# Paired score tiles, a bias table that carries its mask, another order of experts and fewer transposes in a two-layer diffusion backbone

## The chip, the cores and the metric

The kernel runs on one core of a Trainium2 chip. The metric is the device time of one execution in microseconds (us), the median of three runs. The profile is of one further execution of the same program.

## The reference, cut to what matters

Two layers act on 256 latent tokens and 256 context tokens of width 1024, in float32. Each layer has attention heads and state-space (SSD) heads side by side, and then a channel mixer: a dense SwiGLU in layer 0, the two best of eight SwiGLU experts in layer 1. In layer 1 only the latent tokens are needed.

```python
# attention, 8 heads of 64; the grid of latent tokens is 4 rows of 64 columns
s_loc = q_row @ k_halo * scale + bias       # learned bias by row and column distance
s_loc = where(in_win, s_loc, -inf)          # a window of 16 columns, clipped at the edges
s_ctx = q_row @ k_ctx * scale
p = softmax(concat([s_loc, s_ctx]))         # context tokens read context only
# experts, width 3584
combine = softmax(top2(h @ router))         # 0 for the six that a token does not take
for e in range(8):
    out += combine[..., e:e+1] * ((silu(h @ wg[e]) * (h @ wu[e])) @ wd[e])
```

The weights of one expert are 3 x 1024 x 3584 float32, 44.04 MB.

## The kernel before, in words

Instructions outside the experts' loop are ordered by a planner that simulates a timeline; there, the order of the code is only a wish. In the experts' loop the order on TensorE is that of the code. DMAs are issued by SP in one queue, in order.

**The mixer** of a layer projects keys, values, queries and the SSD inputs (`mixer`), and then weaves three generators: `attention`, `ssd` and a filler, which in both layers multiplies the modulation weights `w_mod` (2 MB loads `wm`, L266, matmuls L272). One yield of `attention` covers two scores.

`scores` computes for one head and 128 queries the 256 (context) or 512 (latent) scores into a PSUM bank (`s`, L829; the tag S has two banks), adds the bias for the latent keys on VectorE (L833), takes the maximum (L835) and the exponential with its sum on ScalarE (L837). Head h contracts over partitions 0 to 63 or 64 to 127, as h is even or odd. `flip` transposes the result (L845, copied at L846), `values` multiplies it with the values for two heads (L856) and scales.

The bias of a latent head is read from a table in DRAM, `rscr`. `rpb_scratch` fills it: zeros first (L427), and then, when they have landed, eight DMAs (L429), one for each head, that write the 31 biases of each distance for each of 64 columns in a layout whose rows are shifted by one element against each other. `rpb_tile` loads the tile of one head by two DMAs (L439) and adds the window's mask on GpSimd (L440), a sum of 128 x 384 elements. A tile takes part in the scores of two blocks of queries.

**The experts** (`jobs`). A router sorts the experts by their number of tokens: turn 0 is expert 0 and the others follow by rank. Tokens are gathered by a matmul into `xe` (`slots`, L1309). The expert of rank 1, the largest, has 192 slots and is the side job; the others have 64 each, but rank 0 and 7 have 32 and rank 2 has 96 (a tile of 64 and one of 32). A job runs through its 3584 columns in blocks of 1024, 1024, 1024 and 512; the side job in seven chunks of 512 columns, which are put between the blocks at the places that the list `after` names. In a block TensorE does the first half of gate and up (`gu`, L1339), transposes the hidden values of the block before (`flip`, L1406, evacuated at L1410), does the second half, and then multiplies with the down weights of the block before (`y`, for the side job `ys`, both L1339). `act` (L1390, L1391) makes the hidden values, 64 partitions by 512 columns for each 512 columns of gate; the upper 64 partitions of PSUM hold the up half, so that gate and up run beside each other. A job that is done is scaled (`evac`) and brought back to its tokens by `scatter`: for each tile of slots it splits the result in two parts (`split`), multiplies (L1481) and adds four pieces of 128 x 512 on VectorE (L1492), through two PSUM banks.

The weights pass through 15 buffers of 1 MB, in the order of use (`moe_raw`, L1269 and L1277): a load waits until the matmuls of the load 15 places before it are done. The last block of the last job is written out by hand after the loop, with the final norm (`scatter_last`, `last_norm`).

Of the kernel before, what the change touches and what calls it, by code (L numbers as in the profile page):

```python
# [9 lines left out]
F32 = mybir.dt.float32  # L10
# [28 lines left out]
def constants():  # L39
# [27 lines left out]
C_ID, C_LE, C_LT, C_GE, C_GT, C_ONE, C_MASK = 0, 128, 256, 384, 512, 640, 768  # L67
NB = 1
C_COS, C_SIN, C_PERM, C_IOTA, C_TRI8, C_END = 832, 1088, 1344, 1472, 1728, 1792
# [5 lines left out]
class Build:  # L75
# [87 lines left out]
    def setup(self, es):  # L163
# [15 lines left out]
        cA = cst.tile([P, C_MASK], F32, name="cA")  # L179
        nc.sync.dma_start(cA, a["consts"][:, :C_MASK])  # L180
# [426 lines left out]
    def mixer(self, l, m, esm, es_live, mix, fill, before_lat=None, keys=None):  # L607
# [15 lines left out]
        cB = lp.tile([P, C_IOTA - C_MASK], F32, name=f"cB{l}")  # L623
        cmask = cB[:, 0:64]
        lv.update(cos=cB[:, 64:320], sin=cB[:, 320:576], perm=cB[:, 576:704])

        with ExitStack() as es:
# [26 lines left out]
            with self.tc.issue_after(self.last_load.ins):  # L654
                nc.sync.dma_start(cB, a["consts"][:, C_MASK:C_IOTA])
# [45 lines left out]
        with ExitStack() as es:  # L701
            wk = self.pool(es, f"wk{l}", 2)
            self.use_banks(HB, HT)
            self.weave((self.attention(l, wk, qT, kT, v, cmask, mix, tts, q0), 8 * len(tts) // 2 + 1),
# [1166 lines left out]
```

## Time and profile before

| | before |
|---|---|
| median of 3 runs | 1862.05 us (1859.15 to 1862.22) |
| the profiled execution's own time | 1863.58 us |
| its span, first to last instruction | 1861.8 us |
| PE, PEld, DVE, ACT, POOL busy | 95%, 57%, 39%, 26%, 12% of the span |
| mean granted TensorE clock | 0.966 |
| read from HBM | 496.86 MB |

PE is TensorE's matmuls, PEld its weight loads, DVE VectorE, ACT ScalarE, POOL GpSimd, SP the queue that issues most DMAs. L12 is line 12 of the kernel. A tile's name stands without its number. The matmuls of a float32 product are two instructions, and their records overlap, so that a busy share of PE near 100% is no proof that it is the limit; the chain of work that ended last says more. In the stages' times below, layer 0's weave runs from about 184 to 304 us, layer 1's from 868 to 948 us, and the experts from 1005 us to the end.

### The profile page before, as it was taken

Reading aid. Unit: us, or ns where it says so; the run is one execution under the profiler, and the core shown is the slowest. Engines: PE = TensorE matmul, PEld = TensorE weight load, DVE = VectorE, ACT = ScalarE, POOL = GpSimd, SP = SyncE. Lnnn points to the kernel's source line nnn. Section 1 sums busy time; section 2 is a strip of 40 time slices with the busy share of each in tenths; the row PEclk is TensorE's granted clock in tenths of the full one; section 3 lists DMA queues with packets and bytes.
Section 4 is the critical chain, followed back from the end, with each engine's and each line's share of the span. In section 5 each row is a group of like instructions: output and inputs, shape, how many; then the busy total and the mean of one; then the engine's idle time right before and its main releaser. Section 6 shows DMA issues by size and latency. Waiting matters only on the chain.

```text
span 1861.8 us, 25835 instructions
## 1 busy us (share of the span) xinstructions
PE 1776.7 (95%) x10324; PEld 1063.0 (57%) x10324; DVE 724.6 (39%) x1280; ACT 481.2 (26%) x878; POOL 215.1 (12%) x218
## 2 busy tenths in 40 slices
PE   6999998999999999999898999999999999999996
PEld 4787446798989899886465433433433434334332
DVE  4356485772434378677576102011101111110124
ACT  1333544353222235544342111100100101001011
POOL 2000651330000052303312000000000000000000
PEclk8999998999999999999897999999999999999997
DMA  9643893132213212255857999999999999999996
GB/s 329 186 131 127 320 308 114 68 115 87 103 62 132 90 51 93 95 195 201 298 204 293 409 409 412 411 414 411 410 417 409 411 414 414 408 415 356 390 362 263
DMA packets 176160, 499.78 MB, mean 268 GB/s; under 512 B 32520, under 2 KB 43328, under 8 KB 161760
## 3 DMA queue, kind: packets, MB, share of 16 engines
q1 hardware_dynamic: 175008, 496.26, 70.2%
q8 instruction: 83, 1.36, 0.3%
q10 hardware_dynamic: 608, 1.58, 0.2%
q0 software_dynamic: 416, 0.21, 0.1%
q14 instruction: 45, 0.37, 0.1%
HBM read 496.86 MB, written 4.73 MB: 269 GB/s over the span
## 4 chain that ended last, share of the span: by engine, by line
PE 88%; DVE 5%; DMA 4%; ACT 1%; issue 1%; POOL 0%; SPq 0%; DVEq 0%; ACTq 0%; POOLq 0%
PE gu L1339 25%; PE y L1339 9%; PE fm L455 7%; PE fm L454 7%; PE fm L456 7%; PE ys L1339 4%; PE tm L454 3%; PE tm L455 3%; PE tm L456 3%; PE fo L456 2%; PE fo L455 2%; PE fo L454 2%; DMA mg<-in_moe_w_up_dram 2%; PE s L829 2%; PE hT L1406 2%; PE xe L1309 2%
## 5 line engine op out<-in xcount | busy, mean ns | idle before, releaser
L454 PE MATMUL fm<-mhi,uh 128*128 128x512 f32 (+1 forms) x768 | 265.6, 348 | 7.9 <-ACT uh L127 5.5
L455 PE MATMUL fm<-mlo,uh 128*128 128x512 f32 (+1 forms) x768 | 265.8, 347 | 7.2 <-DVE mlo L400 7.2
L456 PE MATMUL fm<-mhi,ul 128*128 128x512 f32 (+1 forms) x768 | 264.6, 346 | 0.0
L455 PEld LDWEIGHTS fm<-mlo,uh 128*128 128x128 f32 x768 | 147.5, 192 | 27.5 <-DVE mlo L400 10.2
L454 PEld LDWEIGHTS fm<-mhi,uh 128*128 128x128 f32 x768 | 146.9, 192 | 28.4 <-ACT uh L127 6.0
L456 PEld LDWEIGHTS fm<-mhi,ul 128*128 128x128 f32 x768 | 147.3, 192 | 18.3 <-DVE ul L132 0.8
L1391 DVE TENSOR_TENSOR ht<-ht,gu 64x512 f32<-64x512 f32 (+1 forms) x47 | 31.6, 673 | 316.7 <-ACT ht L1390 316.5
L1339 PE MATMUL gu<-mg,xes__8789 128*64 128x512 f32 x624 | 149.2, 594 | 1.0 <-DMA mg<-in_moe_w_up_dram 1.0
L1339 PE MATMUL y<-md,hht 128*32 128x256 f32 (+1 forms) x1024 | 150.0, 506 | 0.0
L921 POOL TENSOR_TENSOR mv<-mv,mhalf 128x1 f32<-128x1 f32 x12 | 8.7, 738 | 962.9 <-DVE mv L920 962.6
L1339 PEld LDWEIGHTS y<-md,hht 128*32 128x32 f32 (+1 forms) x1024 | 51.3, 128 | 97.0 <-issue 86.5
L1410 ACT ACTIVATE hht<-hT 128x256 f32<-128x256 f32 (+1 forms) x47 | 17.6, 376 | 336.1 <-PE hT L1406 334.6
L1339 PEld LDWEIGHTS gu<-mg,xes__8789 128*64 128x64 f32 x624 | 48.6, 137 | 87.5 <-issue 83.8
L454 PE MATMUL fo<-uh,hh 128*128 128x256 f32 (+1 forms) x336 | 95.1, 285 | 0.0
L455 PE MATMUL fo<-ul,hh 128*128 128x256 f32 (+1 forms) x336 | 94.8, 284 | 0.0
L456 PE MATMUL fo<-uh,hl 128*128 128x256 f32 (+1 forms) x336 | 92.3, 285 | 0.0
L1391 DVE TENSOR_TENSOR hs<-hs,gu 64x512 f32<-64x512 f32 x21 | 14.5, 689 | 184.7 <-ACT hs L1390 184.7
L1339 PE MATMUL gu<-mg,xet__11435 128*64 128x512 f32 (+2 forms) x416 | 71.2, 565 | 0.0
L455 PEld LDWEIGHTS fo<-ul,hh 128*128 128x128 f32 x336 | 63.2, 188 | 0.8
L454 PEld LDWEIGHTS fo<-uh,hh 128*128 128x128 f32 x336 | 63.0, 188 | 0.8
L1339 PE MATMUL ys<-md,hhs 128*64 128x512 f32 x288 | 63.0, 594 | 0.0
L456 PEld LDWEIGHTS fo<-uh,hl 128*128 128x128 f32 x336 | 62.0, 188 | 0.7
(442 smaller groups left out, 2953.9 us busy)
## 6 DMA issues: line engine op xcount, KB each, us to landing
mg<-in_moe_w_up_dram SPq DMA_DIRECT2D x65, 1024.0 KB, 15.0
mg<-in_moe_w_gate_dram SPq DMA_DIRECT2D x62, 1024.0 KB, 16.8
md<-in_moe_w_down_dram SPq DMA_DIRECT2D x53, 1024.0 KB, 16.5
md<-in_moe_w_down_dram SPq DMA_DIRECT2D x82, 512.0 KB, 11.9
wm<-in_w_mod_dram SPq DMA_DIRECT2D x20, 2048.0 KB, 10.3
mg<-in_moe_w_gate_dram SPq DMA_DIRECT2D x70, 512.0 KB, 11.1
mg<-in_moe_w_up_dram SPq DMA_DIRECT2D x68, 512.0 KB, 12.3
mraw<-in_moe_w_down_dram SPq DMA_DIRECT2D x18, 1024.0 KB, 13.3
```

What stands on the lines that cost most here:

```text
L454: nc.tensor.matmul(ps, ah, bh, start=first and i == 0, stop=False)
L455: nc.tensor.matmul(ps, ah, bl, start=False, stop=False)
L456: nc.tensor.matmul(ps, al, bh, start=False, stop=last and i == n - 1)
L829: nc.tensor.matmul(sv, qT[hp, h // 2, tt * P - q0:(tt + 1) * P - q0], kT[hp, h // 2, :nk * P], start=True, stop=True)
L921: self.last_pow = nc.gpsimd.tensor_tensor(mv[:, 2:3], mv[:, 2:3], self.mhalf[:, 0:1], op=OP.pow)
L1309: nc.tensor.matmul(tp[:, m * W:(m + 1) * W], M["xn"][i][:, j * P:(j + 1) * P], pick[i][:, :, 0:W // n], start=(i == 0), stop=(i == 1))
L1339: self.last_mm = self.nc.tensor.matmul(o[n * g:n * g + n, :w.shape[1]], x, w, start=first, stop=last)
L1391: nc.vector.tensor_tensor(h, h, o[64:, :w], op=OP.mult)
L1406: self.last_flip = nc.tensor.transpose(tp[:, jj * 64:(jj + 1) * 64], h[:, c0:c0 + 255:2], self.ident[:64, :64])
L1410: nc.scalar.activation(t[:, :n], tp[:, :n * 64].rearrange("p (j s) -> p j s", j=n), AF.Copy)
```

## The change

Four edits. The window's mask moves into the table: `rscr` is filled with -1e30, each of eight DMAs writes the 16 biases of the window for the 49 inner columns, and 15 more DMAs write the edge columns; the sum on GpSimd goes. Scores are made for two heads at a time, in one tile of two PSUM banks of which there is one (tag S, bufs 1), with one bias sum and one maximum for both. In the experts' loop two hidden halves share a tile of 128 partitions, which is transposed at once, and in `scatter` tiles of one size are summed in PSUM before the four sums on VectorE. The ranks are taken in another order, and the chunks of the side job stand at other places.

```diff
-    c = np.arange(GRID)
-    start = np.clip(c - WIN // 2, 0, GRID - WIN)
-    inside = (c[None, :] >= start[:, None]) & (c[None, :] < start[:, None] + WIN)
-    mask = np.where(inside, 0.0, NEG).astype(np.float32)
-    cols.append(np.concatenate([mask, mask], axis=0))
...
     def rpb_scratch(self, l):
 
         nc, a = self.nc, self.a
         W = RHD * RW + 1
         flat = self.rscr[l].rearrange("(c x) -> c x", x=W)
-        src = a["na_rpb"][l, :, 4:11, :].rearrange("h r m -> h (r m)").partition_broadcast(64)
+        grid = self.rscr[l][0:64 * RHD * RW].rearrange("(c r w) -> c r w", c=64, w=RW)
+        bias = a["na_rpb"][l, :, 4:11, :]
+        lo, hi = WIN // 2, GRID - WIN // 2 + 1
         with self.tc.issue_after(self.last_load.ins):
-            nc.sync.dma_start(self.rscr[l], a["zeros"])
+            nc.sync.dma_start(self.rscr[l], a["below"])
             for h in range(8):
                 nc.sync.dma_start(
-                    flat[:, h * 7 * RW:(h + 1) * 7 * RW].rearrange("c (r w) -> c r w", w=RW)[:, :, 0:31],
-                    src[:, h, :].rearrange("c (r m) -> c r m", m=31))
-
-    def rpb_tile(self, l, h, pool, cmask):
+                    flat[lo:hi, h * 7 * RW:(h + 1) * 7 * RW].rearrange("c (r w) -> c r w", w=RW)[:, :, 7:23],
+                    bias[h, :, 7:23].partition_broadcast(hi - lo))
+            for c in [*range(lo), *range(hi, GRID)]:
+                k0 = 0 if c < lo else GRID - WIN
+                m0 = k0 - c + 15
+                nc.sync.dma_start(grid[c, :, 15 + k0:15 + k0 + WIN].rearrange("(h r) w -> h r w", h=8),
+                                  bias[:, :, m0:m0 + WIN])
+    def rpb_tile(self, l, h0, pool):
         nc = self.nc
-        t = pool.tile([P, 6, GRID], F32, tag="bias", bufs=3, name=f"bias{l}{h}")
+        t = pool.tile([P, 2, 6, GRID], F32, tag="bias", bufs=2, name=f"bias{l}{h0}")
         flat = self.rscr[l][0:64 * RHD * RW].rearrange("(c r w) -> c r w", c=64, w=RW)
-        for ii in range(2):
-            r0 = h * 7 + 1 - ii
-            nc.sync.dma_start(t[ii * 64:(ii + 1) * 64], flat[:, r0:r0 + 6, 15:79])
-        nc.gpsimd.tensor_tensor(t, t, cmask[:, None, :].to_broadcast([P, 6, GRID]), op=OP.add)
+        for hh in range(2):
+            for ii in range(2):
+                r0 = (h0 + hh) * 7 + 1 - ii
+                nc.sync.dma_start(t[ii * 64:(ii + 1) * 64, hh], flat[:, r0:r0 + 6, 15:79])
         return t
...
+        def scores(lat, tt, h0, bias, sm):
             nk = 4 if lat else 2
-            hp = slice((h % 2) * HD, (h % 2 + 1) * HD)
-            s = self.bank("s")
-            sv = s[:, :nk * P]
-            nc.tensor.matmul(sv, qT[hp, h // 2, tt * P - q0:(tt + 1) * P - q0], kT[hp, h // 2, :nk * P],
-                             start=True, stop=True)
+            self.uid += 1
+            s = self.ps.tile([P, 2, 512], F32, tag="S", bufs=1, name=f"s{self.uid}")
+            for hh in range(2):
+                hp = slice(hh * HD, (hh + 1) * HD)
+                nc.tensor.matmul(s[:, hh, :nk * P], qT[hp, h0 // 2, tt * P - q0:(tt + 1) * P - q0],
+                                 kT[hp, h0 // 2, :nk * P], start=True, stop=True)
             if lat:
                 o0 = 2 if tt == 2 else 0
-                nc.vector.tensor_tensor(sv[:, 256:], sv[:, 256:],
-                                        bias[:, o0:o0 + 4, :].rearrange("p r c -> p (r c)"), op=OP.add)
-            nc.vector.tensor_reduce(sm[:, 0, h:h + 1], sv, AX.X, OP.max, negate=True)
-            p = wk.tile([P, 512], F32, tag="p", bufs=4, name=f"p{l}{tt}{h}")
-            nc.scalar.activation(p[:, :nk * P], sv, AF.Exp, bias=sm[:, 0, h:h + 1],
-                                 accum_out=sm[:, 1, h:h + 1])
-            return p
+                sl = s[:, :, 256:].rearrange("p h (r c) -> p h r c", c=GRID)
+                nc.vector.tensor_tensor(sl, sl, bias[:, :, o0:o0 + 4, :], op=OP.add)
+            nc.vector.tensor_reduce(sm[:, 0, h0:h0 + 2], s[:, :, :nk * P], AX.X, OP.max, negate=True)
+            ps = []
+            for hh in range(2):
+                h = h0 + hh
+                p = wk.tile([P, 512], F32, tag="p", bufs=4, name=f"p{l}{tt}{h}")
+                nc.scalar.activation(p[:, :nk * P], s[:, hh, :nk * P], AF.Exp, bias=sm[:, 0, h:h + 1],
+                                     accum_out=sm[:, 1, h:h + 1])
+                ps.append(p)
+            return ps
...
+                items += [(pair, h0, i) for h0 in range(0, 8, 2) for i in range(2)]
         sms, ps, pTs = {}, {}, {}
-        for n in range(len(items) + 2):
+        for n in range(len(items) + 1):
             if n < len(items):
-                pair, h, i = items[n]
+                pair, h0, i = items[n]
                 lat = pair[0] == 2
                 tt = pair[i]
                 if (tt,) not in sms:
                     sms[(tt,)] = wk.tile([P, 2, 8], F32, tag=f"sm{tt % 2}", name=f"sm{l}{tt}")
                 if i == 0 and lat:
-                    bias = self.rpb_tile(l, h, wk, cmask)
-                ps[n] = scores(lat, tt, h, bias if lat else None, sms[(tt,)])
-            if 0 <= n - 1 < len(items):
-                pair, h, i = items[n - 1]
-                if i == 0:
-                    pTs[h % 2] = self.sp.tile([P, 4, 256], F32, tag="whi", name=f"pT{l}{pair[0]}{h}")
-                flip(pair[0] == 2, h, i, ps.pop(n - 1), pTs[h % 2])
-                if h % 2 and i:
-                    values(pair, h - 1, dict(pTs))
-            if n % 2 == 1:
-                yield
+                    bias = self.rpb_tile(l, h0, wk)
+                ps[n] = scores(lat, tt, h0, bias if lat else None, sms[(tt,)])
+            if n:
+                pair, h0, i = items[n - 1]
+                for hh, p in enumerate(ps.pop(n - 1)):
+                    if i == 0:
+                        pTs[hh] = self.sp.tile([P, 4, 256], F32, tag="whi", name=f"pT{l}{pair[0]}{h0 + hh}")
+                    flip(pair[0] == 2, h0 + hh, i, p, pTs[hh])
+                if i:
+                    values(pair, h0, dict(pTs))
+            yield
...
+            hs, n = [], 0
             for s, two in zip(J["tiles"], os):
                 w = 512 if s == 64 else blk[1] // 2
                 for o in two:
-                    self.uid += 1
-                    h = pj.tile([P, 512], F32, tag="h", bufs=3, name=f"h{J['nm']}{self.uid}")[:64, :w]
+                    if n % 2 == 0 or w < 512:
+                        self.uid += 1
+                        t = pj.tile([P, 512], F32, tag="h", bufs=2, name=f"h{J['nm']}{self.uid}")
+                        hs.append((t, w, []))
+                        n = 0
+                    h = t[n * 64:n * 64 + 64, :w]
                     nc.scalar.activation(h, o[:64, :w], AF.Silu)
                     nc.vector.tensor_tensor(h, h, o[64:, :w], op=OP.mult)
-                    hs.append(h)
+                    hs[-1][2].append(n)
+                    n += 1
             return hs
+            flipped = []
+            for h, w, ns in hs:
+                tp = self.tbank("hT")
+                m, k = 64 * len(ns), w // P
+                for jj in range(k):
+                    c0 = jj // 2 * 256 + jj % 2
+                    self.last_flip = nc.tensor.transpose(tp[:, jj * m:(jj + 1) * m], h[:m, c0:c0 + 255:2],
+                                                         self.ident[:m, :m])
+                self.uid += 1
+                t = pj.tile([P, 4, P], F32, tag="hh", bufs=2, name=f"hh{J['nm']}{self.uid}")
+                nc.scalar.activation(t[:, :k, :m], tp[:, :k * m].rearrange("p (j s) -> p j s", j=k), AF.Copy)
+                flipped += [t[:, :, n * 64:n * 64 + 64] for n in ns]
...
         def scatter(J):
-            for q, (s, y, pT) in enumerate(zip(J["tiles"], J["ys"], J["pT"])):
-                hl = split(y, f"{J['nm']}{q}")
+            for s in (64, 32):
+                qs = [q for q, w in enumerate(J["tiles"]) if w == s]
+                if not qs:
+                    continue
+                hl = [split(J["ys"][q], f"{J['nm']}{q}") for q in qs]
                 for i in range(2):
                     os = [self.tbank("sc") for _ in range(2)]
-                    back(os, s, pT, i, hl, True, True)
+                    for n, q in enumerate(qs):
+                        back(os, s, J["pT"][q], i, hl[n], n == 0, n == len(qs) - 1)
                     for half, o in enumerate(os):
                         hs = slice(half * 512, (half + 1) * 512)
                         nc.vector.tensor_tensor(acc[i][:, hs], acc[i][:, hs], o, op=OP.add)
...
-        after = [(0, 1), (0, 2), (1, 1), (2, 1), (3, 1), (4, 1), (6, 0)]
+        after = [(0, 1), (0, 2), (3, 3), (4, 3), (5, 0), (5, 2), (6, 0)]
...
-                              for p in [3, 4, 5, 6, 2, 7, 1]]
+                              for p in [4, 2, 3, 5, 7, 6, 1]]
                 with tc.issue_after(gate.ins), tc.issue_after(powed.ins), \
                         tc.manual_schedule(engines={mybir.EngineType.PE}):
-                    ranks = [0, 3, 4, 5, 6, 2, 7]
+                    ranks = [0, 4, 2, 3, 5, 7, 6]
                     self.jobs(M, [(turn[t], p, {0: 32, 2: 96, 7: 32}.get(p, 64), bt) for t, p in enumerate(ranks)], J0,
                               (turn[7], 1, 192, bt), self.last_norm)
```

Not shown: the constants and `cB` lose the 64 columns of the mask, the input `zeros` becomes `below`, and `split` has three buffers in place of two.

## Rows read from the trace of the kernel before

**Rows 1.** Windows: start:end, length, busy per engine, PE clock, DMA share, GB/s.

```profile
237.00:304.00 67.00, 63.64 (x347) 34.59 (x346) 50.64 (x116) 31.49 (x83) 27.93 (x30) 0.95 0.68 221
868.00:892.00 24.00, 14.51 (x82) 5.07 (x82) 13.40 (x11) 10.63 (x29) 23.85 (x18) 0.85 0.96 351
892.00:948.00 56.00, 56.00 (x287) 28.32 (x287) 33.86 (x72) 20.45 (x49) 13.81 (x19) 0.94 0.58 195
...
1122.00:1607.00 485.00, 476.04 (x2284) 180.99 (x2282) 66.15 (x132) 49.93 (x106) 0.00 (x0) 0.99 1.03 412
...
1680.00:1740.00 60.00, 59.75 (x450) 22.76 (x453) 4.28 (x9) 6.80 (x16) 0.00 (x0) 0.97 0.93 352
...
1780.00:1800.00 20.00, 19.95 (x164) 8.01 (x166) 2.28 (x4) 1.74 (x4) 0.00 (x0) 0.85 0.81 302
```

**Rows 2.** The chain that ended last, in order of time: start, length, what.

```profile
183.93 1.85 PE mod L272 x16
...
228.95 0.63 PE s L829 x2
...
267.48 1.91 PE s L829 x4
...
1165.39 10.30 PE gu L1339 x48
...
1228.64 1.10 PE hT L1406 x8
...
1247.68 7.02 PE gu L1339 x32
...
1501.01 16.39 DMA mg<-in_moe_w_up_dram
...
1826.48 5.44 PE y L1339 x64
```

**Rows 3.** Instructions on the scores' tile: ns min/median/max, first and last start, forms.

```profile
L835 DVE TENSOR_REDUCE sm<-s x48: 408/678/692, 189.2 to 946.1; 128x1 f32<-128x512 f32 x32, 128x1 f32<-128x256 f32 x16
L837 ACT ACTIVATE p<-s,sm x48: 457/681/688, 190.3 to 946.9; 128x512 f32<-128x512 f32 x32, 128x256 f32<-128x256 f32 x16
L837 ACT ACTIVATION_READ_ACCUMULATOR p<-s,sm x48: 188/193/212, 190.7 to 947.5; 128x1 f32 x48
L833 DVE TENSOR_TENSOR s<-s,bias x32: 410/424/433, 239.1 to 945.6; 128x256 f32<-128x256 f32 x32
```

**Rows 4.** Timeline of TensorE at the side job's scatter: start, length, what.

```profile
1814.26 0.51 PE L1481 MATMUL sc<-yhs,pTs 64*128 64x512 f32 x2
1814.60 0.40 PE L1481 MATMUL sc<-yls,pTs 64*128 64x512 f32 x2
```

**Rows 5.** Timeline at the start of layer 1's weave.

```profile
869.81 1.98 PE L829 MATMUL s<-kT,qT 64*128 64x512 f32 x4
...
883.15 1.45 POOL L440 TENSOR_TENSOR bias<-bias,cB 128x384 f32<-128x384 f32 x1
```

**Rows 6.** Timeline of SP's queue around the two bias tables.

```profile
82.03 6.85 SPq L429 DMA_DIRECT2D rscr<-in_na_rpb_dram  x8
90.41 0.38 SPq L446 DMA_DIRECT2D wv<-in_w_in_dram  x1
...
105.94 7.23 SPq L429 DMA_DIRECT2D rscr<-in_na_rpb_dram  x8
113.27 0.64 SPq L266 DMA_DIRECT2D wm<-in_w_mod_dram  x1
```

**Rows 7.** Instructions on the values' weights in layer 0.

```profile
L127 ACT ACTIVATE uh<-wv x4: 1044/1056/1067, 144.3 to 160.3; 128x1024 fp32r<-128x1024 f32 x4
```

**Rows 8.** Gate and up of the last three experts: first and last start.

```profile
L1339 PE MATMUL gu<-mg,xet__10886 x192: 592/593/644, 1486.4 to 1599.8; 128*64 128x512 f32 x192
L1339 PE MATMUL gu<-mg,xet__11435 x416: 378/592/644, 1607.1 to 1726.9; 128*64 128x512 f32 x65, 128*32 128x512 f32 x52, 128*32 128x256 f32 x22
L1339 PE MATMUL gu<-mraw,xet__12006 x24: 592/592/617, 1738.5 to 1809.5; 128*32 128x512 f32 x24
```

More of the change, by code (lines that the diff above doesn't have):

```diff
@@ L178, in setup @@
         tmp = self.pool(est, "stmp", 1, side="right")
-        cA = cst.tile([P, C_MASK], F32, name="cA")
-        nc.sync.dma_start(cA, a["consts"][:, :C_MASK])
+        cA = cst.tile([P, C_COS], F32, name="cA")
+        nc.sync.dma_start(cA, a["consts"][:, :C_COS])
         self.ident = cA[:, C_ID:C_ID + P]
@@ L622, in mixer @@
                   dte=lp.tile([P, 2, 4, 8], F32, name=f"dte{l}"))
[L623 to L625 removed]
+        cB = lp.tile([P, C_IOTA - C_COS], F32, name=f"cB{l}")
+        lv.update(cos=cB[:, 0:256], sin=cB[:, 256:512], perm=cB[:, 512:640])
         with ExitStack() as es:
@@ L703, in mixer @@
             self.use_banks(HB, HT)
-            self.weave((self.attention(l, wk, qT, kT, v, cmask, mix, tts, q0), 8 * len(tts) // 2 + 1),
+            self.weave((self.attention(l, wk, qT, kT, v, mix, tts, q0), 8 * len(tts) // 2 + 1),
                        (self.ssd(l, wk, lv, dtt, mix, tts), 7 + 6 * len(tts)),
@@ L873, in attention @@
             if pair[0] in tts:
-                items += [(pair, h, i) for h in range(8) for i in range(2)]
+                items += [(pair, h0, i) for h0 in range(0, 8, 2) for i in range(2)]
         sms, ps, pTs = {}, {}, {}
-        for n in range(len(items) + 2):
+        for n in range(len(items) + 1):
             if n < len(items):
-                pair, h, i = items[n]
+                pair, h0, i = items[n]
                 lat = pair[0] == 2
@@ L1391, in act @@
                     nc.vector.tensor_tensor(h, h, o[64:, :w], op=OP.mult)
-                    hs.append(h)
+                    hs[-1][2].append(n)
+                    n += 1
             return hs
         def flip(J, blk, hs):
-            out, hs = [], iter(hs)
-            for s in J["tiles"]:
-                hT = []
-                for _ in range(blk[1] // 512 if s == 64 else 1):
-                    h = next(hs)
-                    n = h.shape[1] // P
-                    tp = self.tbank("hT")
-                    for jj in range(n):
-                        c0 = jj // 2 * 256 + jj % 2
-                        self.last_flip = nc.tensor.transpose(tp[:, jj * 64:(jj + 1) * 64], h[:, c0:c0 + 255:2],
-                                                             self.ident[:64, :64])
-                    self.uid += 1
-                    t = pj.tile([P, 4, 64], F32, tag="hh", bufs=4, name=f"hh{J['nm']}{self.uid}")
-                    nc.scalar.activation(t[:, :n], tp[:, :n * 64].rearrange("p (j s) -> p j s", j=n), AF.Copy)
-                    hT.append(t)
+            flipped = []
@@ L1412, in flip @@
+            out = []
+            for s in J["tiles"]:
                 if s == 64:
+                    hT = [flipped.pop(0) for _ in range(blk[1] // 512)]
                     out.append(lambda t, odd, hT=hT: hT[t // 2][:, t % 2 * 2 + odd, :])
                 else:
-                    m = n // 2
-                    out.append(lambda t, odd, hT=hT, m=m: hT[0][:, t % m * 2 + odd, t // m * 32:t // m * 32 + 32])
+                    hT, m = flipped.pop(0), blk[1] // 512
+                    out.append(lambda t, odd, hT=hT, m=m: hT[:, t % m * 2 + odd, t // m * 32:t // m * 32 + 32])
@@ L1855 @@
     arrays, aps = {}, {}
-    for name in _INS + ["consts", "zeros"]:
+    for name in _INS + ["consts", "below"]:
         if name == "consts":
             arr = constants()
-        elif name == "zeros":
-            arr = np.zeros(64 * (RHD * RW + 1), np.float32)
+        elif name == "below":
+            arr = np.full(64 * (RHD * RW + 1), NEG, np.float32)
         else:
```

14 lines of the change are left out of this document (6 added, 8 removed).

## Prediction, made before the changed kernel ran

> **What bounds the kernel now.** I read the chain of waits that ended last first, then the windows by stage, then the tiles that the change touches.
>
> The chain [rows 2] is TensorE nearly throughout. In the experts its last DMA is the one at 1501.01 us; from there to the end it holds TensorE and, at the scatters, VectorE. The windows show the other side [rows 1]: from 1122 to 1607 us the DMA share is 1.03 at 412 GB/s. The experts are thus balanced between two limits. One expert's 44.04 MB take 44.04 / 0.412 = 106.9 us, a side chunk's 6.29 MB take 15.3 us, together 122.2 us; TensorE's period for a 64-slot expert with one chunk is 1607.1 - 1486.4 = 120.7 us [rows 8]. After 1607 us the balance breaks. The expert with 96 slots takes 1738.5 - 1607.1 = 131.4 us [rows 8] for 106.9 us of weights, its buffers fill, and the DMA rate falls to 352 GB/s over 60 us and to 302 GB/s over 20 us [rows 1]. That is (412 - 352) / 412 x 60 = 8.7 us and (412 - 302) / 412 x 20 = 5.3 us of transfers, 14.0 us in all.
>
> In the weaves TensorE is busy too, but at the start of layer 1's it works 14.51 of 24 us while GpSimd works 23.85 [rows 1]. Its first scores are begun at 869.81 us, and the first sum of the mask on GpSimd comes at 883.15 us [rows 5].
>
> **Scores in pairs.** Two latent score products stand at 1.91 us in the chain, 0.955 us each, and one context product at 0.63 us [rows 2]. Before, neighbours in the order are two blocks of queries of one head, on the same half of the array. After, they are an even and an odd head, on different halves. The nearest row for that is the scatter: two half-height matmuls take 0.51 us together and the next two end 0.74 us after the first began [rows 4], where the second pair's record alone is 0.40 us, so the two of a pair run beside each other. If that holds here, a pair costs what one did: 8 x 0.955 + 8 x 0.63 = 12.7 us less TensorE work in layer 0, 8 x 0.955 = 7.6 us in layer 1. The lower bound is 0, if they queue.
>
> The price is the one score tile. The next pair's product must wait until both exponentials of this pair are done. The sum grows from 0.424 to about 0.69 us (256 more columns cost 0.678 - 0.408 = 0.27 us in the maximum's two forms), the maximum to 0.678 + 2 x 0.27 = 1.22 us, the exponentials are 2 x (0.681 + 0.193) = 1.75 us [rows 3]. With the product of 0.95 us this is 4.6 us; I take 5 us with the hand-offs. Layer 0's latent half has 67 / 8 = 8.4 us for a pair, layer 1 after 892 us has 56 / 8 = 7.0 us [rows 1]. So the chain of a pair fits, but not with much room in layer 1, and transposes, values, SSD and modulation matmuls must fill the gap. VectorE saves about 0.3 us a pair.
>
> **The mask.** It takes the sum on GpSimd away, 1.45 us for the first [rows 5], less where GpSimd is alone. In layer 0, where GpSimd works 27.93 of 67 us [rows 1] and VectorE is ahead of it, the slack covers it: 0; without that cover it would be the 1.45 us of each of eight sums. In layer 1 the first softmax no longer waits behind GpSimd's queue; of the 24 - 14.51 = 9.5 us in which TensorE is idle there I take 4, bounds 0 and 9.5, because SSD's own sums hold GpSimd too.
>
> **The tables.** 15 more DMAs are issued by SP for each layer, at 6.85 / 8 = 0.86 us [rows 6], so 12.9 us. The values' load moves from 90.41 to 103.3 us; its weights are first used at 144.3 us [rows 7]. The first `wm` behind the second table moves from 113.27 to 139 us; its matmuls are at 183.93 us [rows 2]. Cost 0, hidden by these 45 us. One head more of bias loads than before goes ahead of the `wm` loads at each weave's start, since two pairs are fetched in place of three heads: two DMAs, 1 to 2 us, taken off below.
>
> **Sum of the weaves.** Layer 0: 12.7 us of TensorE work less, of which I let 8 through, since VectorE works 50.64 of 67 us there [rows 1] and the pair's chain passes it twice. Layer 1: 7.6 + 4 - 1.6 = 10 us. Bounds: 0 and 12.7, 0 and 17. What they save moves all that follows, and so the weight stream of the experts.
>
> **Transposes and scatter.** Eight transposes take 1.10 us, 0.1375 each [rows 2]. Three blocks of 1024 columns need four in place of eight for each 64 slots, 3 x 4 x 0.1375 = 1.65 us for each of five experts; a chunk eight in place of twelve, 0.55 us for each of seven: 12 us less TensorE work, if a transpose of 128 rows costs what one of 64 does. The side job's scatter runs from 1814.26 to 1826.48 us [rows 4, 2], 12.2 us, because twelve sums on VectorE through two banks hold TensorE. Four are left; I take half, 6 us. Both count only where TensorE, not the DMA, is last.
>
> **The order.** A chunk is 144 matmuls, 48 of which take 10.30 us [rows 2], and 12 transposes: 30.9 + 1.65 = 32.6 us. So a 64-slot expert alone is 120.7 - 32.6 = 88.1 us, 86.4 after. Half the matmuls of one, 1.75 blocks of 3 x 7.02 us [rows 2], is 36.9 us; with the 11 us that remain of the 88.1, an expert with 32 slots is about 50 us. The ledger after, TensorE against DMA: second expert 86 to 107, so TensorE waits and the buffers hold no backlog; the 96-slot one 130 to 107, 23 behind; the next two with a chunk 118 to 122, 4 won back each; the 32-slot one with two chunks 114 to 138, 23 won back; the last with a chunk and the side job's scatter about 117 to 122. Fifteen buffers are 15.7 MB, 38 us of transfers, so 23 us of backlog can be taken up in the middle, and nothing is behind at the end. Of the 14.0 us of lost transfers I take 11 back: 1.5 us go to a last expert of 64 slots (its last two loads are 16 matmuls, 3.5 us, in place of half that), 1.5 us to a brim in the 96-slot expert. Bounds 0 and 17, the latter with some of the scatter's saving at the end.
>
> **The sum.** 8 + 10 + 11 = 29 us off the profiled execution's own 1863.58 (its span is 1861.8, 1.8 around it): 1834.6. The median shown is 1.5 us lower, 1862.05, so I say 1834. A change under 0.2%, 3.7 us, can't be told from none here.
>
> **Rivals.**
>
> *The one score tile becomes the limit, slower (chance 0.11).* It decides from 7.0 us a pair in layer 1 and 8.4 us in layer 0. At 9 us, with a VectorE instruction of others ahead of the sum and of the maximum, the cost is 8 x 2.0 = 16 and 8 x 0.6 = 5 us in place of the 18 saved: 1862.05 + 21 - 11 = 1872. For it: VectorE's 50.64 of 67 us. Against it: 5 us without a queue. What would make it bite is that the waiting product holds back what stands behind it on TensorE. The Trainium skill (TensorE: Matmul & The Clock Gate, section Part 3: Packing small matmuls) has matmuls start and end strictly in program order; by that rule every wait for the tile is a wait of the whole queue. No row here shows a matmul that overtook another.
>
> *Only the experts gain (0.14).* The weaves stay on VectorE, GpSimd and the `wm` loads: 1862 - 11 = 1851.
>
> *Only the weaves gain (0.09).* The 96-slot expert fills the buffers in the middle as it did late, and the chunks after it keep them full: 1862 - 18 = 1844.
>
> *The tables come late (0.05).* If a write takes 2.1 us in place of 0.86, 23 take 48 us: the first table ends at 130, the second at about 194 us, and the first `wm` is issued there, 10 us after its use, and needs at least 2.1 MB / 0.412 = 5 us more: 1834 + 15 = 1849. The Trainium skill (DMA: Bandwidth & Descriptors, section Why a DMA increments its semaphore by 16 and not by 1) lets a DMA use the largest number of engines up to 16 that divides its slowest dimension; the 49 columns would go over 7 engines where 64 went over 16, which is how a write could become that slow. The rows have no transfer of 49.
>
> *It does nothing that can be measured (0.05).* 1862.
>
> **How the numbers follow.** The forecast itself has 0.56: its own range is 1817, with all bounds on the good side, to 1848, with half of the sum. The range of 8 in 10 goes on to the cases at 1849 and 1851, with their own spread, and leaves out the slow one and the best end: 1817 to 1856. Faster 0.83 (0.56 + 0.14 + 0.09 + 0.04 of the late tables), same 0.06, slower 0.11.
>
> **What would show it.** Right: latent score products of a pair in 1 us or little more, layer 1's first exponential before 882 us counted from the same start, no window of the experts under 400 GB/s before the last 20 us, and a scatter of the side job of some 6 us. Wrong: TensorE waiting for ScalarE's exponential ahead of scores for more than some 10 us in sum, a second `wm` wait at layer 0's start, or a DMA rate that falls in the 96-slot expert and the chunks behind it.

## The result and the profile after

The changed kernel takes 1830.67 us (median of 4 runs, 1829.24 to 1832.0) where the kernel before takes 1861.88 (median of 4): ratio 0.9835, interval [0.9818, 0.9852], 31 us less. The profiled execution takes 1831.6 us, its span is 1829.8, the mean clock 0.973 (0.966 before).

Windows of the changed kernel for those of [rows 1]. The three of the weaves begin 5 us ahead of their counterparts, since the marks come earlier there; those of the experts stand at the same times as before, and the one from 1620 to 1680 us is added:

```profile
232.00:299.00 67.00, 57.96 (x357) 32.53 (x357) 50.70 (x103) 33.18 (x85) 24.32 (x26) 0.97 0.72 242
863.00:887.00 24.00, 16.53 (x99) 7.10 (x99) 16.21 (x15) 13.03 (x35) 23.04 (x18) 0.90 1.00 332
887.00:934.00 47.00, 45.70 (x290) 25.54 (x290) 31.81 (x62) 20.05 (x50) 8.19 (x12) 0.98 0.81 274
1122.00:1607.00 485.00, 469.66 (x2572) 168.70 (x2569) 65.89 (x124) 46.84 (x91) 0.00 (x0) 0.98 1.03 413
1620.00:1680.00 60.00, 54.77 (x422) 22.55 (x420) 5.88 (x12) 6.42 (x14) 0.00 (x0) 0.91 1.03 410
1680.00:1740.00 60.00, 57.87 (x280) 19.47 (x278) 10.68 (x17) 4.46 (x8) 0.00 (x0) 0.97 1.03 411
1780.00:1800.00 20.00, 19.12 (x98) 7.63 (x98) 3.95 (x6) 1.57 (x4) 0.00 (x0) 1.00 1.03 416
```

TensorE is busy for 57.96 of 67 us in layer 0's half (63.64 before), layer 1's weave after its start is through in 47 us (56 before), and the dips to 352 and 302 GB/s are gone. The chain of waits of the changed kernel, the pieces that answer to [rows 2]:

```profile
1138.75 19.59 DMA md<-in_moe_w_down_dram
...
1172.29 18.88 DMA mg<-in_moe_w_up_dram
...
1227.96 1.30 PE hT L1419 x8
...
1628.90 17.27 DMA mg<-in_moe_w_up_dram
...
1695.24 11.13 DMA mg<-in_moe_w_up_dram
...
1780.31 1.64 PE sc L1497 x12
1783.28 1.67 PE sc L1497 x10
1784.94 7.02 PE y L1349 x32
```

TensorE waits for weights in the second expert and again at 1628.90 and 1695.24 us, the last of them until 1706; before, the last such link ended at 1517 [rows 2]. So the weights set the pace until 189 us later than before. The side scatter takes 1780.31 to 1784.94, 4.6 us (12.2 before), and a transpose of 128 rows 1.30 / 8 = 0.16 us (0.1375 with 64).

### The profile page after: what moved, and what is told of

It reads as the page before. It is cut to its first block, busy times and chain, and to the rows that moved or that the text cites. A ratio compares the mean times of both kernels' runs of the same rounds, so it can differ in the third digit from the quotient of the medians.

```text
span 1829.8 us, 25533 instructions
## 1 busy us (share of the span) xinstructions
PE 1734.6 (95%) x10236; PEld 1037.4 (57%) x10236; DVE 712.8 (39%) x1232; ACT 476.2 (26%) x856; POOL 203.3 (11%) x202
## 4 chain that ended last, share of the span: by engine, by line
PE 84%; DMA 7%; DVE 5%; ACT 1%; POOL 1%; issue 1%; SPq 0%; DVEq 0%; ACTq 0%; POOLq 0%
PE gu L1349 24%; PE y L1349 8%; PE fm L460 7%; PE fm L459 7%; PE fm L461 7%; PE ys L1349 4%; DMA mg<-in_moe_w_up_dram 3%; PE tm L459 3%; PE tm L460 3%; PE tm L461 3%; DMA wm<-in_w_mod_dram 2%; PE fo L461 2%; PE fo L460 2%; PE fo L459 2%; PE xe L1319 2%; PE hT L1419 1%
## 5 line engine op out<-in xcount | busy, mean ns | idle before, releaser
L1349 PE MATMUL gu<-mg,xes__8731 128*64 128x512 f32 x600 | 141.6, 603 | 2.1 <-DMA mg<-in_moe_w_up_dram 1.2
L1423 ACT ACTIVATE hht<-hT 128x512 f32<-128x512 f32 (+2 forms) x32 | 15.0, 473 | 306.4 <-PE hT L1419 306.4
L1349 PEld LDWEIGHTS gu<-mg,xes__8731 128*64 128x64 f32 x600 | 44.7, 139 | 85.5 <-issue 78.9
L1349 PE MATMUL ys<-md,hhs 128*64 128x512 f32 x264 | 59.3, 605 | 0.0
```

The source lines that it names most:

```text
L1349: self.last_mm = self.nc.tensor.matmul(o[n * g:n * g + n, :w.shape[1]], x, w, start=first, stop=last)
L1423: nc.scalar.activation(t[:, :k, :m], tp[:, :k * m].rearrange("p (j s) -> p j s", j=k), AF.Copy)
```

## The experiments

The table gives, for each run, the ratio to the kernel before and the interval, and from its profiled execution (us) the start of layer 0's last exponential, of layer 1's first, of the router's maximum, of the second expert's first matmul, the last weight load issued, and the end of the span. Runs with the same weave differ by up to 4 us in such a mark, so means over them are used below.

| run | ratio | L0 last | L1 first | router | 2nd expert | last load | end |
|---|---|---|---|---|---|---|---|
| before | 1 | 296.8 | 889.7 | 986.3 | 1121.7 | 1822.5 | 1861.8 |
| changed | 0.9835 [0.9818, 0.9852] | 292.8 | 873.0 | 967.3 | 1096.3 | 1785.9 | 1829.8 |
| e1 order alone | 1.0065 [1.004, 1.009] | 298.6 | 888.5 | 985.0 | 1120.5 | 1812.5 | 1865.8 |
| e2 transposes, scatter | 0.9986 [0.9971, 1.0001] | 299.5 | 886.1 | 982.0 | 1116.3 | 1814.1 | 1855.0 |
| e3 mask | 0.9928 [0.9907, 0.9948] | 298.1 | 874.9 | 971.4 | 1101.7 | 1803.6 | 1843.7 |
| e4 pairs | 0.9971 [0.9952, 0.9989] | 293.0 | 886.2 | 978.8 | 1113.9 | 1811.4 | 1850.4 |
| e5 e1 and e2 together | 0.9939 [0.9924, 0.9954] | 299.0 | 889.8 | 986.0 | 1120.2 | 1808.0 | 1851.5 |
| e6 changed, old order | 0.9858 [0.9842, 0.9875] | 291.9 | 871.5 | 966.0 | 1095.2 | 1793.0 | 1833.2 |
| e7 changed, 32 slots last | 0.9836 [0.9823, 0.9849] | 293.2 | 873.0 | 967.7 | 1096.7 | 1790.8 | 1831.1 |
| e8 changed, old scatter | 0.9879 [0.9864, 0.9893] | 293.1 | 873.0 | 967.6 | 1096.7 | 1786.4 | 1837.0 |
| e9 sums held | 0.999 [0.9978, 1.0003] | 298.5 | 886.5 | 982.5 | 1112.6 | 1815.0 | 1854.3 |
| e10 mask, other sums | 0.9924 [0.9911, 0.9936] | 297.3 | 874.6 | 970.7 | 1101.1 | 1802.9 | 1842.2 |
| e11 same half | 0.993 [0.9917, 0.9944] | 301.5 | 882.4 | 983.8 | 1112.9 | 1802.3 | 1846.1 |
| e12 spread | 0.9835 [0.9811, 0.9858] | 294.3 | 875.3 | 969.5 | 1098.6 | 1791.2 | 1829.2 |

**The parts one by one, on the kernel before.** e1 takes these lines of the diff alone:

```diff
-        after = [(0, 1), (0, 2), (1, 1), (2, 1), (3, 1), (4, 1), (6, 0)]
+        after = [(0, 1), (0, 2), (3, 3), (4, 3), (5, 0), (5, 2), (6, 0)]
...
-                    ranks = [0, 3, 4, 5, 6, 2, 7]
+                    ranks = [0, 4, 2, 3, 5, 7, 6]
```

> The kernel before with nothing changed but the order of the experts and the places of the side chunks. Theory (the order recovers the lost transfers): the DMA rate has no dip to 352 and 302 GB/s any more, and of the 14.0 us of lost transfers about 11 come back, less what the old scatter takes at the end, so 8 to 11 us faster, 1851 to 1854. Rival (the experts' gain after is less TensorE work from transposes and scatter, and the order only moves the wait from one expert to another): within 3 us of before.

Measured: 12 us slower (7 to 17). Neither theory held. In the profiles the stream, from the first expert's matmul to the last load issued, is 9 us shorter (991.7 to 1812.5, 820.8 us; before 992.9 to 1822.5, 829.6), but the tail, from there to the end, is 14 us longer (53.3 for 39.3). That makes 5 us and not 12, since the profile before is long in its experts: e3, e4, e9 and e10, which have the same experts, take 825.8 and 39.4 us on average. Against them e1's stream is 5 us shorter and the whole 9 us longer. The rates show that part of the dips came back in the middle, windows of e1:

```profile
1500.00:1560.00 60.00, 59.80 (x302) 24.23 (x300) 5.74 (x14) 7.11 (x16) 0.00 (x0) 1.00 1.02 402
1620.00:1680.00 60.00, 58.13 (x445) 23.80 (x446) 7.04 (x13) 6.82 (x15) 0.00 (x0) 1.00 0.98 390
```

and its chain has the last wait for weights here, so that TensorE sets the end from 1732 us on:

```profile
1720.90 11.16 DMA mg<-in_moe_w_up_dram
...
1819.72 8.24 PE y L1339 x32
```

e2 takes `act`, `flip`, `split` and `scatter` of the change alone:

```diff
-                for i in range(2):
-                    os = [self.tbank("sc") for _ in range(2)]
-                    back(os, s, pT, i, hl, True, True)
+                    for n, q in enumerate(qs):
+                        back(os, s, J["pT"][q], i, hl[n], n == 0, n == len(qs) - 1)
```

> The kernel before with nothing changed but the transposes of two halves at once and the side tiles summed in PSUM. Theory: these count only where TensorE is last. From 1607 us on in the kernel before it is, and there lie the scatter (12.2 us, 4.6 in the changed kernel) and some 1.35 + 2 x 0.3 us of transposes; 8 to 10 us faster at most, 1852 to 1854, and little on top of the new order. Rival (transposes and scatter run beside VectorE and DMA waits that stay): within 3 us of before.

Measured: 2.6 us less (0 to 5), the rival's size. In the kernel before TensorE holds the chain from 1517 us on, so a shorter scatter should count there. But in e2 TensorE comes through the scatter early and then waits for the last weights. Its waits from 1800 to 1835 us (us in total, times, longest):

```profile
PE y L1339 <- DMA md<-in_moe_w_down_dram: 2.3, 2, 1.4
PE y L1339 <- DMA mraw<-in_moe_w_down_dram: 2.0, 2, 1.3
PE gu L1339 <- DMA mg<-in_moe_w_up_dram: 1.0, 1, 1.0
```

That is 5.3 us of the 7.6 that the scatter is shorter; the kernel before has no such wait there. The stream keeps its dips in the old order (373 GB/s over 1680 to 1740 us) and ends no sooner.

e3 takes the mask table, with single scores:

```diff
-        nc.gpsimd.tensor_tensor(t, t, cmask[:, None, :].to_broadcast([P, 6, GRID]), op=OP.add)
```

> The kernel before with nothing changed but the mask written into the table, so that GpSimd adds none; scores one by one in two score tiles as before. Theory (both weave parts count, the mask only at layer 1's start): layer 0 unchanged, layer 1's first exponential 4 to 8 us earlier, 4 to 5 us faster in all, about 1857. Rival (the mask alone makes the weaves' gain, because GpSimd's queue held the first softmax and the wait ran through the whole of layer 1): 12 us or more faster, 1850 or less. Second rival (GpSimd's sums of SSD hold the first softmax anyway): within 2 us.

Measured: 13 us faster, the rival's size. Layer 1's first exponential comes 14.8 us earlier and the router's maximum 14.9; layer 0 is unchanged.

e4 takes the paired scores, with the mask still on GpSimd:

```diff
+        nc.gpsimd.tensor_tensor(t, t, cmask[:, None, None, :].to_broadcast([P, 2, 6, GRID]), op=OP.add)
```

> The kernel before with nothing changed but the scores of two heads at once in one tile; the mask is still added on GpSimd, one sum of 128x768 for a pair, and the first pair waits for it. Theory (paired products free TensorE in both layers): 5 us in layer 0, 6 to 8 us in layer 1 less 1 to 2 us because the first mask sum is twice as long, in all 9 to 12 us faster, 1850 to 1853. Rival (the paired scores gain nothing without the mask table, since GpSimd's sum stands before each pair): within 3 us of before or slower.

Measured: 5.4 us faster (2 to 9), between theory and rival. Layer 0 has its 5 us; what layer 1 gains does not stand out of the spread of the marks.

The four parts alone sum to +0.65 - 0.14 - 0.72 - 0.29 = -0.50%, 9 us; together they give -1.65%, 31 us. So some of them depend on each other.

**Together, and one at a time out of the changed kernel.** e5 is the kernel before with the edits of e1 and e2:

> The kernel before with the new order, the transposes of two halves and the summed scatter together; the weaves are those of before. Theory (they only pay together: the order shortens the weight stream by some 9 us but leaves a last expert of 64 slots and the side scatter behind it, 53 us from the last weight load issued to the end in place of 39; transposes and scatter take that tail back): from the first expert's matmul to the end 856 us as in the changed kernel, where the kernel before took 869 and the order alone 874; about 13 us faster, 1847. Rival (the terms add, +5 and -3): within 4 us of before.

Measured: 11.4 us faster (9 to 14), the theory: +12 and -3 become -11. From the last load issued to the end 43.5 us are left of e1's 53.3. e6 is the changed kernel with the first lines of e1's diff as they stand before:

> The changed kernel with the order of the experts and the places of the chunks of before. Theory (with short transposes and the short scatter the new order is worth 866 - 856 = 10 us, by the experts' time of the run with these two alone): 8 to 11 us slower than the changed kernel, about 1840. Rival (the order is worth nothing or costs, as alone): 1825 to 1833.

Measured: 4.3 us slower than the changed kernel (0.9858 against 0.9835), half of the theory's. With the new scatter and transposes the order gains; with the old ones it costs. As in e2, TensorE waits for the last weights, 5.7 us from 1780 us on. e8 puts the old `split` and `scatter` into the changed kernel:

> The changed kernel with the side tiles scattered one by one as before. Theory (the side scatter lies in the tail, where TensorE is last, and took 12.2 us against 4.6): 7 to 8 us slower than the changed kernel, 1838. Rival (the tail has room for it, or the weight stream is last): within 2 us of the changed kernel.

Measured: 8.2 us slower (0.9879 against 0.9835), the theory. Timeline of TensorE in e8: the first of six such pairs, the start of the second, which waits for VectorE's sums, and the end of the last:

```profile
1778.26 0.50 PE L1497 MATMUL sc<-yhs,pTs 64*128 64x512 f32 x2
1778.60 0.40 PE L1497 MATMUL sc<-yls,pTs 64*128 64x512 f32 x2
1780.49 1.10 PE L1497 MATMUL sc<-yhs,pTs 64*128 64x512 f32 x2 [1.50 <-DVE res L1508]
...
1789.24 1.21 PE L1497 MATMUL sc<-yls,pTs 64*128 64x512 f32 x2
```

Nothing that issues weights is held up there: the last load leaves at 1786.4 us, 812.2 after the first expert's matmul, as in the changed kernel (811.9). From it to the end it takes 50.6 us in place of 43.9.

**Two other orders.** e7 exchanges the last two experts of the changed kernel:

```diff
-                    ranks = [0, 4, 2, 3, 5, 7, 6]
+                    ranks = [0, 4, 2, 3, 5, 6, 7]
```

> The changed kernel with the last two experts exchanged, so that the 64-slot one with two chunks comes first and the 32-slot one with one chunk is last. Theory (what is left of the experts is the tail: 44 us from the last weight load issued to the end, of which an expert of 32 slots would need some 10 less): the weight stream keeps its 411 GB/s, TensorE waits for weights in the last expert, and the kernel is 5 to 10 us faster than the changed one, 1821 to 1826. Rival (the 64-slot expert with two chunks, 86 + 62 = 148 us of TensorE for 138 us of weights, fills the buffers and the stream stalls before the last expert): within 3 us of the changed kernel or slower.

Measured: as the changed kernel, the rival. From the last load to the end it takes 40.3 us, 3.6 less, but the 64-slot expert with two chunks fills the buffers, and the stream takes 816.4 us in place of 811.9. Windows of e7:

```profile
1560.00:1620.00 60.00, 58.41 (x275) 20.05 (x271) 8.08 (x12) 4.53 (x8) 0.00 (x0) 1.00 0.97 386
...
1680.00:1740.00 60.00, 60.00 (x314) 20.48 (x312) 7.64 (x11) 5.44 (x11) 0.00 (x0) 1.00 0.97 385
```

e12 exchanges them too and moves chunks, so that the second expert has one:

```diff
-        after = [(0, 1), (0, 2), (3, 3), (4, 3), (5, 0), (5, 2), (6, 0)]
+        after = [(0, 1), (0, 2), (1, 1), (3, 3), (4, 3), (5, 1), (6, 0)]
```

> The changed kernel with the order of experts in which the second one, where TensorE waits for weights, gets a chunk, the expert with 32 slots is last, and none has two chunks but the first: no expert after the one of 96 slots is heavier on TensorE than on the weights, and the last has 86 us of work for 122 us of weights. Theory (the weight stream at its full rate, some 812 us from the first expert's matmul to the last load issued, and 40 us behind it as in the run with the 32-slot expert last): 1824 to 1828, 2 to 6 us faster than the changed kernel. Rival (the 96-slot expert now meets full buffers, since TensorE no longer waits ahead of it, and the stream stalls there): the changed kernel's 1830 or slower.

Measured: 0.9835 again, with a wider interval. Its experts take 853.1 us in place of 855.8 in the profiles, less than the runs can tell. In e7 and e12 TensorE waits for weights 8.2 and 11.7 us from 1750 us on, in the changed kernel 0.5 us from 1690 us on: there the stream sets the end. No version run here beats the changed kernel.

**Why the mask table gains in layer 1.** e10 is e3 with other sums on GpSimd, meant to stand in place of the mask's:

```diff
+        nc.gpsimd.tensor_tensor(self.junk, self.cA[:, 0:384], self.cA[:, 0:384], op=OP.add)
```

> The kernel with the mask table and single scores, as in the third run, and in place of each mask sum a GpSimd sum of the same size, 128x384, into a tile that nothing reads. Theory (layer 1's first softmax waited for the mask sum that stood behind SSD's in GpSimd's queue): the first exponential of layer 1 stays at 875 to 878 us and the router's maximum at 972 to 975, where before they are at 889.7 and 986.3. Rival (the gain is GpSimd's time, which SSD needs): they go back to 885 or later and 982 or later. The first expert's period, 123.7 us in the third run, says in either case whether GpSimd's last sums meet the routing again.

Measured: 0.9924 and 874.6 us, the whole gain. But the run does not decide between theory and rival. Nothing waits for these sums, and the planner put all 16 at the start of the kernel, far ahead of the weaves; the row of e10:

```profile
L446 POOL TENSOR_TENSOR junk<-cA x16: 826/828/1787, 7.2 to 34.6; 128x384 f32<-128x384 f32 x16
```

So e10 is e3 a second time, and the question is left to the timelines. VectorE's at the first bias sum, in the changed kernel:

```profile
864.17 3.81 DVE L787 TENSOR_TENSOR E<-E 128x512 f32<-128x512 f32 x2 [1.79 <-POOL E L775]
870.94 0.70 DVE L840 TENSOR_TENSOR s<-s,bias 128x512 f32<-128x512 f32 x1 [2.95 <-DMA bias<-rscr]
871.67 1.23 DVE L841 TENSOR_REDUCE sm<-s 128x2 f32<-128x1024 f32 x1
```

and in the kernel before:

```profile
879.69 2.37 DVE L783 TENSOR_TENSOR E<-E 128x512 f32<-128x512 f32 x1 [6.78 <-POOL E L771]
...
887.34 0.75 DVE L833 TENSOR_TENSOR s<-s,bias 128x256 f32<-128x256 f32 x2
```

Now VectorE waits only for the table's rows, 6 us after the first score product (864.9); before, the sum came 17.5 us after it, behind SSD's sums and the mask. GpSimd's second pair of SSD sums in the kernel before:

```profile
877.77 3.75 POOL L771 TENSOR_TENSOR E<-E,cs 128x1024 f32<-128x1024 f32 x2
```

and in e3:

```profile
876.74 3.74 POOL L773 TENSOR_TENSOR E<-E,cs 128x1024 f32<-128x1024 f32 x2
```

Up to these sums GpSimd does the same work in both, 1.0 to 1.1 us apart; the first mask sum of the kernel before follows at 883.15 us [rows 5], and e3 has its first exponential at 874.9 us. So the early first softmax is not GpSimd's time: it no longer stands behind other work. The eight mask sums of this weave are 8.8 us of GpSimd's time, and how much of the gain behind the first softmax comes from them, no run separates.

**What a pair's products are worth.** e11 lets both products of a pair read the lower half.

```diff
-                hp = slice(hh * HD, (hh + 1) * HD)
+                hp = slice(0, HD)
```

> The changed kernel, with both score products of a pair read from the lower half of the partitions, so that the second repeats the first's head and half of the heads are left out. Theory (the two products of a pair run beside each other because they are on different halves of the array): two latent products take 1.1 us in place of some 0.6, the weave of layer 0 ends 3 to 5 us later, layer 1's 0 to 4 us, 1834 to 1838 in all. Rival (layer 0's gain comes from fewer and longer VectorE instructions, not from TensorE): within 2 us of the changed kernel.

Measured: 17.7 us slower than the changed kernel (0.993 against 0.9835), more than either. The 1.1 and 0.6 us expected for two products were both too small. One latent pair in TensorE's timeline, in the changed kernel:

```profile
269.63 1.13 PE L835 MATMUL s<-kT,qT 64*128 64x512 f32 x4
```

and in e11:

```profile
269.81 1.98 PE L835 MATMUL s<-kT,qT 64*128 64x512 f32 x4
```

So the two halves run beside each other, 0.85 us saved a latent pair: 13.6 us for 16 pairs. Eight context pairs add 3.4 us (1.13 us for a pair in e11, 0.70 in the changed kernel). Against the mean of the five runs with the changed weave (293.1, 873.2, 967.6) layer 0 ends 8.4 us later and layer 1's part behind it takes 16.2 - 8.4 = 7.8 us more. About all that TensorE does longer comes out at the end.

**The first expert.** In the kernel before it takes 1121.7 - 992.9 = 128.8 us, in the changed one 122.3. VectorE's timeline in the kernel before:

```profile
993.14 1.30 DVE L1230 TENSOR_TENSOR sw<-oh,ci 128x64 f32<-128x64 f32 x1
994.36 0.15 DVE L1245 TENSOR_TENSOR cap<-cap,few 128x8 f32<-128x8 f32 x1
994.47 0.22 DVE L1231 TENSOR_REDUCE key<-sw 128x8 f32<-128x64 f32 x1
994.61 1.11 DVE L1244 TENSOR_SCALAR few<-rank 128x8 f32<-128x8 f32 x1
```

and GpSimd's:

```profile
991.72 2.63 POOL L1803 TENSOR_TENSOR res<-xn,res 128x512 f32<-128x512 f32 x2 [6.77 <-PE xe L1309]
994.43 2.61 POOL L1803 TENSOR_TENSOR res<-res,res 128x512 f32<-128x512 f32 x2
```

The routing, on which SP waits for the next weights, is drawn out while GpSimd's sums run. e9 holds these back until the routing is done:

```diff
+                    held = nc.gpsimd.tensor_copy(hold, self.routed[:, 1])
...
-                        with tc.issue_after(self.last_pooled.ins):
+                        with tc.issue_after(held.ins):
```

> The kernel before, with the eight GpSimd sums of the last layer's residual held behind the end of VectorE's routing by one small copy on GpSimd that reads the routing's last result. Theory (in the kernel before these sums begin 5.4 us after the router's maximum and VectorE's routing instructions then take 1.06 to 1.30 us in place of 0.15 to 0.22; in the changed kernel the sums begin 9.0 us after it, when the routing is nearly done, by the luck of a later transfer): the routing ends some 6 us earlier, SP issues the next weights 5 to 6 us earlier, the first expert's period falls from 128.8 to 122 or 123 us, and the kernel is 5 to 6 us faster, 1856. Rival (the long instructions wait for something else, and the changed kernel's short first period comes from the weight stream): within 2 us of before.

Measured: the first expert's period falls to 123.5 us as expected, but the time only by 0 to 4 us, nearer to the rival's. VectorE in e9, with GpSimd waiting:

```profile
990.12 0.16 DVE L1245 TENSOR_SCALAR few<-rank 128x8 f32<-128x8 f32 x1
990.24 0.22 DVE L1237 TENSOR_TENSOR sw<-oh,comb 128x64 f32<-128x64 f32 x1
```

What e9 gains at the start it gives back late, where full buffers stop the stream (346 GB/s over 1660 to 1700 us, 378 before): e4, whose first expert takes 128.5 us, needs 865.0 us from that expert's first matmul to the end, e9 865.2. With the old order and the old scatter the end is TensorE's; the chain of e9 has no wait for weights after 1508 us.

## Why the prediction came out, step by step

**Weaves, 8 and 10 us: right in sum, wrong in their parts.** Over the five runs with the old weave the three marks are 298.5, 888.1 and 984.4 us, with the changed one 293.1, 873.2 and 967.6: layer 0 gives 5.4, layer 1 another 11.4, together 16.8 for 18 forecast. The products on two halves are worth what "Scores in pairs" said: 8 let through in layer 0 (8.4 by e11) and 7.6 in layer 1 (7.8). The step that failed is the price of pairing, which "So the chain of a pair fits" set at 0. The pairs as a whole give 5 us in layer 0 (e4) and nothing in layer 1 (e3 and e10 reach the router's maximum 13.3 us early, the changed weave 16.8, and 5.4 of that is layer 0's). So pairing costs about 3 and 8 to 10 us beside what the products give.

The windows show the price as idle time of TensorE. Layer 0's weave, before and after:

```profile
184.00:304.00 120.00, 114.14 (x622) 57.42 (x617) 79.55 (x171) 57.23 (x164) 60.82 (x63) 0.96 0.77 264
184.00:300.00 116.00, 102.03 (x631) 52.32 (x630) 80.22 (x151) 59.63 (x170) 56.12 (x55) 0.97 0.80 274
```

TensorE is busy 12.1 us less, near the 12.7 of the prediction, but idle 14.0 us in place of 5.9. Layer 1 from the first score to the router, with the mask table and single scores (e3) and in the changed kernel:

```profile
867.00:971.00 104.00, 96.89 (x536) 56.56 (x536) 72.78 (x149) 47.38 (x106) 32.57 (x34) 0.98 0.85 288
863.00:967.00 104.00, 91.68 (x537) 54.88 (x536) 71.71 (x133) 47.25 (x107) 33.69 (x34) 0.97 0.85 300
```

Here TensorE is busy 5.2 us less and idle 5.2 us more, so nothing is left. What it waits for in the changed kernel (us in total, times, longest), in layer 0 and then in layer 1:

```profile
PE pT L855 <- ACT p L846: 5.8, 5, 2.3
...
PE st L726 <- POOL xe L722: 3.9, 2, 2.6
PE pT L855 <- ACT p L846: 2.7, 3, 1.3
```

In layer 0 the transposes `pT` wait 5.8 us for the exponentials (1.4 before). In layer 1 a product of SSD, `st`, waits 3.9 us for GpSimd's `xe`, which it does not in e3, and the transposes 2.7 (1.4 in e3). The next pair's scores wait for ScalarE only 1.7 us in both layers. So the wait that the prediction priced, for the tile, is small, and the cost lies in what comes behind the scores. Whether the pairs' longer instructions or the planner's new order make these waits stays open. In layer 1 a pair takes (930.1 - 873.0) / 7.5 = 7.6 us in the changed kernel, over the 7.0 from which that rival decides; by single scores two take 6.8 (874.9 to 925.6, e3), but e3 then needs 45.8 us more to the router's maximum, the changed kernel 37.2. The rule of the Trainium skill beside that rival (TensorE: Matmul & The Clock Gate, section Part 3: Packing small matmuls), strict program order, was not tested: no run tells where a waiting product held back others.

**The mask, 4 us in layer 1 with bounds 0 to 9.5: mis-sized, and over its bound.** It is worth 13.3 (e3, e10). The bound took TensorE's idle time at the start, but the first softmax came 11.5 us too late, and what hangs on it (transposes, values, SSD between them) followed. From the first score to the router in the kernel before:

```profile
868.00:986.00 118.00, 104.17 (x537) 58.58 (x536) 74.42 (x149) 48.23 (x107) 40.72 (x42) 0.93 0.76 273
```

In e3, above, TensorE is idle 6.7 us less (7.1 for 13.8), and its matmuls, as many, take 7.3 us less at a granted clock of 0.98 in place of 0.93. For the clock the sum had no term. The two errors, mask too small and pairs too good, cancel; that the weaves' sum came out is luck.

**Tables, 0: right.** SP's queue in the changed kernel:

```profile
82.19 6.85 SPq L428 DMA_DIRECT2D rscr<-in_na_rpb_dram  x8
89.09 10.27 SPq L434 DMA_DIRECT2D rscr<-in_na_rpb_dram  x15
99.46 0.39 SPq L451 DMA_DIRECT2D wv<-in_w_in_dram  x1
...
130.49 0.39 SPq L261 DMA_DIRECT2D wm<-in_w_mod_dram  x1
```

A write of 49 columns is issued in 6.85 / 8 = 0.86 us, as one of 64 was [rows 6], and an edge write in 10.27 / 15 = 0.68 us; `wv` goes at 99.46 and `wm` at 130.49, 45 and 53 us ahead of 144.3 and 183.93 [rows 7, 2]. Over how many DMA engines a write of 49 columns goes, the rule of the Trainium skill weighed there (DMA: Bandwidth & Descriptors, section Why a DMA increments its semaphore by 16 and not by 1), no run shows.

**Experts, 11 us: right as a sum, 11.4 by e5; the step that failed is where it comes from.** The order was to recover 11 us of lost transfers by itself and the shorter scatter and transposes to count little. By e1 the order alone costs 12: the stream is 5 to 9 us shorter, and "1.5 us go to a last expert of 64 slots" was 14 with the old scatter behind it and still 4 to 5 with the new (43.5 us in e5, 43.9 in the changed kernel, 39.3 before). TensorE sets the end from 1732 us on in e1, so there the scatter's 7.6 us (8.2 by e8) and the transposes count. Only with them is the order a gain of 4 to 9 us (e6; e5 against e2), and only with the order are they more than 2.6 us (e2). The remark that scatter and transposes "count only where TensorE, not the DMA, is last" was right, and not followed to its end: the new order makes that place, while in the old one TensorE waits for the last weights as soon as the scatter is short.

**The signs.** All four came: 1.13 us a latent pair, the first exponential at 873.0 us, no window of 60 us behind 1020 us under 400 GB/s, a scatter of 4.6 us (6 said, so the saving is 7.6 in place of 6). Of the signs of being wrong none came. The chain has a second `wm` link in layer 0, at 224.75 us, but TensorE does not wait for it: it is busy all 20 us from 220 to 240.

## What to carry to other kernels

A reorder that evens out a weight stream is judged with the tail that it leaves: the work behind the last load counts in full, so shorten that work first. Parts tested alone can have the wrong sign; here the order cost 12 us alone and gained with its partners. A sum on a side engine is priced by who waits for it and what then comes late, before that engine's time. A dummy instruction that nothing waits for may run anywhere: look in the trace where it ran before it is called a test (e10).

## What was not expected of the hardware

In the kernel before, eight of VectorE's small instructions in the routing, one for each of GpSimd's eight 128x512 sums (1.27 us each by median), took 1.06 to 1.30 us in place of 0.15 to 0.23; those that fell between two sums were short, and all were when the sums were held back (e9). The reductions beside them stayed at 0.22. The Trainium skill (SBUF — State Buffer, section SBUF: two separate sides) has VectorE and GpSimd share one pair of ports as an exclusive lock, held for a whole instruction, in VectorE's fast modes or with two inputs from SBUF; by that rule each such VectorE instruction waits for the sum that runs, and the rows agree, its 1.1 to 1.3 us with the 1.27. In the changed kernel the collision is mostly missed, since the sums begin 9.0 us after the router's maximum in place of 5.4, released by a later transfer:

```profile
976.33 2.62 POOL L1824 TENSOR_TENSOR res<-xn,res 128x512 f32<-128x512 f32 x2 [10.31 <-DMA res<-in_ln_g_dram]
```

It is a side effect of other timing, not of an edit.
